# A column mean over 8192 rows: wider adds at the start, and another split of the last rows between VectorE and TensorE

## The chip, the cores and the metric

The kernel runs on one core of a Trainium2 chip. Times are device microseconds (us) of one execution. The median of three runs of the kernel before is 630.81 us (630.23 to 630.88). The execution whose trace is read here took 630.37 us, and its span, from the first to the last instruction that the profiler recorded, is 628.5 us.

## The reference

```python
def setup_inputs():
    return {"x": np.random.randn(8192, 8192).astype(np.float32)}

def reference(x: np.ndarray) -> np.ndarray:
    return np.mean(x, axis=0)
```

The input has 268.44 MB in HBM, and each number is needed once. The result is one row of 8192 numbers (32 KB).

## The kernel before, in words

**Tiles.** The 8192 rows are 64 groups of 128 rows (`G` is 64, `P` is 128). A group fills one slot of 128 partitions x 8192 columns of fp32. The tile `bufs` has six such slots. Slots 0 to 3 are landing places; slot 4 is called `both`, and slot 5 is `acc`, the accumulator. Columns are counted in blocks of 512 (`F`), so a group has 16 blocks. A small tile `early` holds 6 blocks.

**Loads.** SyncE (SP) issues every load, in program order, on one queue (line 52). Groups come in pairs: one DMA of 8.39 MB fills two neighbouring slots with 64 KB for each partition (`load_rows`). Pair `g` goes to slots `u` and `u + 1`, `u = (g + 2) % 4`, so that two pairs can be in flight or in use. The first pair goes straight to slots 4 and 5. A load into a slot waits for the add that read the slot last. The first six blocks of group 60 are loaded ahead of their turn, into `early`: two blocks as the first DMA of all, four more behind pair 4 (`load_early`). Helper `load` makes every second load wait besides for the loads eight and seven places earlier (`over`).

**Adds.** VectorE works in the order of the program. For pairs 2 and 4 there is one double add, `sums2 += two slots`, 16384 columns wide, which treats `both` and `acc` as one. After pair 4, `acc += both`. From pair 6 on, every pair has two adds of 8192 columns: `both = slot + slot`, then `acc += both`. Pair 58 is the last. An add that waits for a load has a no-op in front of it on ScalarE, or for two adds in eight on GpSimd, which waits for the load and for the add ahead (line 75), so that VectorE waits for a single semaphore. GpSimd adds the early blocks into `acc` after pairs 24 and 32 (line 110).

**The last four groups** come one by one and in pieces. For groups 60 and 61, VectorE adds blocks 6 to 15 to `acc` (5120 columns each). Group 62 comes as blocks 0 to 5 and 6 to 15; VectorE adds blocks 6 to 11 of it (3072 columns). Group 63 comes in four pieces, of 8, 4, 3 and 1 blocks. The names are `r60` to `r63`.

**The sum over partitions** is TensorE's (line 154). A matmul with a 128x32 tile of 1/8192 sums 512 columns over the partitions and adds the result to a PSUM bank. Block `i` goes to bank `i // 4`, and in it to column group `q = i % 4` of the array (32 of its 128 columns), by `tile_position`. What was not added on VectorE is given to TensorE as it is: `blocks(r62, 0, 6)` are six matmuls, one for each block. The last four blocks (2048 columns) are treated in another way: `chunks(row, 0, 3)` are four matmuls of 384 columns, one for each column group, with three quarters of these blocks' columns block by block, into bank 3; `chunks(row, 3, 4)` are four of 128 columns into bank 4. TensorE takes its matmuls in the order of the list `sums`, and the first matmul that has to wait for something holds the rest.

**The end.** ScalarE copies banks 0, 1, 2 and 3 to SBUF (line 167) and issues the store of bank 0 behind the first copy. VectorE copies bank 4 (line 177). SyncE stores banks 1 and 2, then banks 3 and 4 (line 170). Between these, SyncE has no-ops that wait for things that are long done (`landed`), so that the program's end needn't wait for all of them at once. A last no-op on VectorE waits for the first store (`hold`).

Of the kernel before, what the change touches and what calls it, by code (L numbers as in the profile page):

```python
# [9 lines left out]
def kernel(  # L10
# [5 lines left out]
    nc = tc.nc  # L16
    f32 = mybir.dt.float32
    M, N = x.shape
    P = nc.NUM_PARTITIONS
    F = 512  # L20
# [3 lines left out]
    sync = mybir.DependencyInfo(mybir.DependencyClass.Sync, mybir.DependencyReason.DATA)  # L24
# [6 lines left out]
    acc = bufs[:, U - 1, :]  # L31
    ones = sb.tile([P, 32], f32, name="ones")
    E = 6
# [2 lines left out]
    warm = sb.tile([P, 32], f32, name="warm")  # L36
    nc.gpsimd.memset(ones[:], 1.0 / M)  # L37
    ready = sb.tile([P, 1], f32, name="ready")
    set_up = tc.keep_in_program_order(
        nc.gpsimd.tensor_add(out=ready[:], in0=ones[:, 0:1], in1=ones[:, 1:2])).ins  # L40
    banks = [psp.tile([P, F], f32, name=f"bank{b}") for b in range(5)]

    loads = []

    def landed(*inss):

        nop = tc.keep_in_program_order(nc.sync.nop()).ins
        for o in inss:
            tc.add_manual_dep(nop, o.name, sync, reason="SyncE waits")

    def load(dst, src):
        ins = tc.keep_in_program_order(nc.sync.dma_start(out=dst, in_=src)).ins  # L52
        k = len(loads)
        over = loads[k - 8:k - 6] if k >= 8 and k % 2 == 0 else []
        tc.declare_no_dep(ins, group="loads", keep=over, reason="the reader of the buffer waited")
        for o in over:
            tc.add_manual_dep(ins, o.name, sync, reason="covers the next load too")
        tc.add_to_no_dep_group("loads", ins)
        loads.append(ins)
        return ins  # L60

    def rows(g, n=1):
        return x[g * P:(g + n) * P, :]

    def load_rows(g, u, n):
        return load(bufs[:, u:u + n, :], rows(g, n).rearrange("(p j) c -> p j c", j=n))
# [3 lines left out]
    def add(dst, a, b, dmas):  # L70

        ins = tc.keep_in_program_order(nc.vector.tensor_add(out=dst, in0=a, in1=b)).ins  # L72
        if dmas:
            waiter = nc.scalar if len(adds) % 8 > 1 else nc.gpsimd
            nop = joins[waiter] = tc.keep_in_program_order(waiter.nop()).ins  # L75
            for o in dmas + adds[-1:]:
                tc.add_manual_dep(nop, o.name, sync, reason="the no-op waits")
            for group in ("loads", "adds"):
                tc.declare_no_dep(ins, group=group, reason="the no-op waited")
            tc.add_manual_dep(ins, nop.name, sync, reason="waits for both at once")  # L80
        elif adds:
            tc.declare_no_dep(ins, group="loads", reason="the add ahead waited")
        tc.declare_no_dep(ins, group="early", reason="the no-op waited, or the add behind it")
        tc.add_to_no_dep_group("adds", ins)
        adds.append(ins)

    def load_early(lo, hi):
        load(early[:, lo * F:hi * F], rows(G - 4)[:, lo * F:hi * F])
# [6 lines left out]
    for g in range(2, G - 4, 2):  # L95
        u = (g + 2) % 4
        dma = load_rows(g, u, 2)
        if g < 6:
            add(sums2, sums2, bufs[:, u:u + 2, :], [dma] + first)
            first = []  # L100
            if g == 4:
                load_early(2, E)
                add(acc, acc, both, [])
            continue
        add(both, bufs[:, u, :], bufs[:, u + 1, :], [dma])
        add(acc, acc, both, ahead)
        ahead = []
        if g in (24, 32):
            cols = slice(0, 2 * F) if g == 24 else slice(2 * F, E * F)
            ins = tc.keep_in_program_order(nc.gpsimd.tensor_add(  # L110
                out=acc[:, cols], in0=acc[:, cols], in1=early[:, cols])).ins
            tc.add_to_no_dep_group("early", ins)
            ahead = [ins]

    r60, r61, r62, r63 = [bufs[:, (G - 4 + 2 + j) % 4, :] for j in range(4)]
    cols = slice(E * F, N)
# [2 lines left out]

    for lo, hi in [(0, 6), (6, 16)]:  # L120
        dma = load(r62[:, lo * F:hi * F], rows(G - 2)[:, lo * F:hi * F])
    cols = slice(6 * F, 12 * F)
    add(acc[:, cols], acc[:, cols], r62[:, cols], [dma])
    for lo, hi in [(0, 8), (8, 12), (12, 15), (15, 16)]:
        load(r63[:, lo * F:hi * F], rows(G - 1)[:, lo * F:hi * F])
# [3 lines left out]
    def blocks(row, lo, hi):  # L129
        for i in range(lo, hi):  # L130
            sums.append((i // 4, i % 4, row[:, i * F:(i + 1) * F]))

    def chunks(row, lo, hi):
        for q in range(4):
            cols = row[:, 12 * F:].rearrange("p (j q w) -> p q j w", j=4, q=4)[:, q, lo:hi, :]
            sums.append((3 + lo // 3, q, cols))
# [1 line left out]
    blocks(r62, 0, 6)  # L138
    blocks(acc, 0, 6)
    blocks(r61, 0, 6)  # L140
    chunks(r62, 0, 3)
    chunks(acc, 0, 3)
    blocks(r63, 0, 6)
    blocks(acc, 6, 12)
    blocks(r63, 6, 12)
    chunks(r62, 3, 4)
    chunks(acc, 3, 4)
    chunks(r63, 0, 3)
    chunks(r63, 3, 4)
    for n, (b, q, cols) in enumerate(sums):  # L150
        dst = banks[b][32 * q:32 * q + 32, :]
        if b > 2:
            dst = dst.rearrange("p (j w) -> p j w", w=W)[:, :cols.shape[1], :]
        summed = tc.keep_in_program_order(nc.tensor.matmul(  # L154
            out=dst,
# [10 lines left out]
    def copy(dst, src):  # L166
        return tc.keep_in_program_order(nc.scalar.copy(out=dst, in_=src)).ins  # L167

    def store(engine, dst, src):
        return tc.keep_in_program_order(engine.dma_start(out=dst, in_=src)).ins  # L170

    copy(res[:, 0, :], banks[0][:])
    s0 = store(nc.scalar, out[:4 * F].rearrange("(q c) -> q c", q=4), res[0:P:32, 0, :])
    for b in (1, 2):
        copy(res[:, b, :], banks[b][:])
    copied = copy(fin[:, :3 * W], banks[3][:, :3 * W])
    ended = nc.vector.tensor_copy(out=fin[:, 3 * W:], in_=banks[4][:, :W]).ins  # L177
    landed(*joins.values())
    landed(loads[-6], set_up)
    landed(*loads[-5:-3])  # L180
    s1 = store(nc.sync, out[4 * F:12 * F].rearrange("(b q c) -> q b c", q=4, c=F), res[0:P:32, 1:3, :])
    landed(copied)
    store(nc.sync, out[12 * F:].rearrange("(j q w) -> q j w", j=4, q=4),
          fin[0:P:32, :].rearrange("q (j w) -> q j w", w=W))
    landed(*loads[-3:-1])
    landed(loads[-1], s0)
    landed(s1, summed)
    landed(ended)
    hold = tc.keep_in_program_order(nc.vector.nop()).ins
    tc.add_manual_dep(hold, s0.name, sync, reason="VectorE ends late")  # L190


# [28 lines left out]
```

## Time and profile before

| | |
|---|---|
| median of three runs | 630.81 us (630.23 to 630.88) |
| the profiled execution's own time | 630.37 us |
| its span | 628.5 us |
| VectorE (DVE) busy | 530.0 us, 84% of the span, 61 instructions |
| TensorE (PE) busy | 15.9 us, 3% |
| ScalarE (ACT), GpSimd (POOL) busy | 3.7 us, 7.3 us |
| read from HBM | 268.44 MB, 427 GB/s over the span |

The page of the profile has busy times, a strip of 40 slices of 15.7 us each, the DMA queues, the chain of work that ended last, and the costliest groups of instructions. Engine names are PE (matmuls), PEld (weight loads), DVE, ACT, POOL and SP; a `q` behind a name is the engine's sequencer, with its waits and DMA issues. A matmul of fp32 is recorded as two, so that 60 matmuls of the program are 120 in the trace.

### The profile page before, as it was taken

What the parts mean: (1) busy time and instruction counts of PE and PEld (TensorE: products, weight loads), DVE (VectorE), ACT (ScalarE), POOL (GpSimd) and SP (SyncE); (2) the same over time, 40 slices, a digit from 0 to 9 for tenths busy, and PEclk for the clock granted to TensorE, in tenths of its full rate; (3) what the DMA queues carried; (4) which work ended last, traced back from release to release, by engine and by line L of the source; (5) the groups of instructions that cost most, each with busy time, mean ns of one, the idle gap of its engine ahead of it and who ended that gap; (6) DMA issues with size and microseconds to landing.
All of it is one profiled execution on the core that took longest, in us unless ns stands there. A gap on an engine that the chain in (4) does not pass through costs nothing.

```text
span 628.5 us, 466 instructions
## 1 busy us (share of the span) xinstructions
PE 15.9 (3%) x120; PEld 4.9 (1%) x120; DVE 530.0 (84%) x61; ACT 3.7 (1%) x6; POOL 7.3 (1%) x8
## 2 busy tenths in 40 slices
PE   0000000000000000000000000000000000000037
PEld 0000000000000000000000000000000000000002
DVE  0028999999888898888988899988889888898895
ACT  0000000000000000000000000000000000000001
POOL 0000000000000000010000200000000000000000
PEclk9999999999999999999999999999999999999999
DMA  8999999999999999999999999999999999999996
GB/s 371 463 400 430 437 467 400 467 400 467 400 467 400 467 400 467 400 467 400 467 400 467 400 467 400 467 400 467 400 467 401 463 405 463 405 463 405 432 418 254
DMA packets 5802, 268.50 MB, mean 427 GB/s; under 512 B 652, under 2 KB 668, under 8 KB 1064
## 3 DMA queue, kind: packets, MB, share of 16 engines
q1 hardware_dynamic: 5792, 268.46, 98.9%
q8 instruction: 1, 0.02, 0.0%
q10 hardware_dynamic: 8, 0.01, 0.0%
q14 instruction: 1, 0.01, 0.0%
HBM read 268.44 MB, written 0.03 MB: 427 GB/s over the span
## 4 chain that ended last, share of the span: by engine, by line
DMA 67%; DVE 28%; another core or an unknown queue 3%; PE 1%; SPq 0%; issue 0%; ACTq 0%; POOLq 0%
DMA bufs<-in_x_dram 67%; DVE bufs L72 28%; PE bank L154 1%; SPq L52 0%; ACTq L75 0%; DVE fin L177 0%; POOLq L75 0%
## 5 line engine op out<-in xcount | busy, mean ns | idle before, releaser
L72 DVE TENSOR_TENSOR bufs<-bufs 128x8192 f32<-128x8192 f32 (+3 forms) x60 | 529.7, 8828 | 90.8 <-POOLq L75 54.2
L154 PE MATMUL bank<-bufs,ones 128*32 128x512 f32 (+2 forms) x120 | 15.9, 588 | 609.5 <-DMA bufs<-in_x_dram 608.9
L110 POOL TENSOR_TENSOR bufs<-bufs,early 128x1024 f32<-128x1024 f32 (+1 forms) x2 | 6.8, 3414 | 350.1 <-DVE bufs L72 350.1
L154 PEld LDWEIGHTS bank<-bufs,ones 128*32 128x32 f32 x120 | 4.9, 118 | 620.3 <-issue 616.5
L167 ACT COPY bufs<-bank 128x512 f32<-128x512 f32 x3 | 1.8, 585 | 620.8 <-PE bank L154 620.8
L177 DVE COPY fin<-bank 128x128 f32<-128x128 f32 x1 | 0.3, 291 | 5.0 <-PE bank L154 5.0
L93 ACT ACT_TABLE_LOAD x1 | 1.3, 1283 | 0.7 <-PEq L205 0.7
L167 ACT COPY fin<-bank 128x384 f32<-128x384 f32 x1 | 0.5, 478 | 0.5 <-PE bank L154 0.5
L93 ACT COPY warm<-ones 128x32 f32<-128x32 f32 x1 | 0.2, 218 | 0.0
L40 POOL TENSOR_TENSOR ready<-ones 128x1 f32<-128x1 f32 x1 | 0.2, 193 | 0.1
L37 POOL MEMSET ones<- 128x32 f32 x1 | 0.1, 124 | 0.3 <-POOLq L205 0.3
L205 POOL MEMSET const-bfloat16-1.0<- 128x1 bf16 x1 | 0.1, 101 | 0.0
L205 POOL MEMSET const-uint8-127<- 128x1 uint8 x1 | 0.1, 101 | 0.0
L205 POOL MEMSET const-float32-0.0<- 128x1 f32 x1 | 0.1, 98 | 0.2 <-issue 0.2
L205 POOL MEMSET const-float32-1.0<- 128x1 f32 x1 | 0.1, 98 | 0.0
## 6 DMA issues: line engine op xcount, KB each, us to landing
bufs<-in_x_dram SPq DMA_DIRECT2D x2, 2560.0 KB, 16.6
bufs<-in_x_dram SPq DMA_DIRECT2D x1, 4096.0 KB
bufs<-in_x_dram SPq DMA_DIRECT2D x1, 2048.0 KB, 20.8
bufs<-in_x_dram SPq DMA_DIRECT2D x1, 1536.0 KB
early<-in_x_dram SPq DMA_DIRECT2D x1, 1024.0 KB, 62.4
bufs<-in_x_dram SPq DMA_DIRECT2D x1, 1024.0 KB, 22.9
bufs<-in_x_dram SPq DMA_DIRECT2D x1, 768.0 KB, 24.2
early<-in_x_dram SPq DMA_DIRECT2D x1, 512.0 KB, 3.4
```

The lines of the kernel that those rows point to most:

```text
L37: nc.gpsimd.memset(ones[:], 1.0 / M)
L40: nc.gpsimd.tensor_add(out=ready[:], in0=ones[:, 0:1], in1=ones[:, 1:2])).ins
L72: ins = tc.keep_in_program_order(nc.vector.tensor_add(out=dst, in0=a, in1=b)).ins
L93: tc.keep_in_program_order(nc.scalar.copy(out=warm[:], in_=ones[:]))
L110: ins = tc.keep_in_program_order(nc.gpsimd.tensor_add(out=acc[:, cols], in0=acc[:, cols], in1=early[:, cols])).ins
L154: summed = tc.keep_in_program_order(nc.tensor.matmul(out=dst, lhsT=ones[:], rhs=cols, start=all(k[:2] != (b, q) for k in sums[:n]), stop=a ...
L167: return tc.keep_in_program_order(nc.scalar.copy(out=dst, in_=src)).ins
L177: ended = nc.vector.tensor_copy(out=fin[:, 3 * W:], in_=banks[4][:, :W]).ins
L205: nc = _bacc.Bacc("TRN2", target_bir_lowering=False, num_devices=1)
```

## The change

In the first part, pairs 2, 4 and 6 are added at double width, and `acc += both` follows pair 6. The four early blocks that came behind pair 4 come as two loads, blocks 2 and 3 behind pair 4, blocks 4 and 5 behind pair 6.

In the last part, VectorE adds blocks 12 to 15 of group 62 to `acc` (2048 columns) instead of blocks 6 to 11. TensorE gets blocks 6 to 11 of group 62 as six matmuls instead of the eight `chunks` of it, so it has 58 matmuls instead of 60, and it takes them in another order. The store of banks 3 and 4 no longer lists ScalarE's copy among its own waits (a no-op ahead of it waits for that copy), one no-op no longer waits for GpSimd's first add, and VectorE's last no-op waits for the store of banks 1 and 2 instead of the store of bank 0.

```diff
-        if g < 6:
+        if g < 8:
             add(sums2, sums2, bufs[:, u:u + 2, :], [dma] + first)
             first = []
-            if g == 4:
-                load_early(2, E)
+            if g > 2:
+                load_early(g - 2, g)
+            if g == 6:
                 add(acc, acc, both, [])
             continue
...
-    cols = slice(6 * F, 12 * F)
+    cols = slice(12 * F, N)
     add(acc[:, cols], acc[:, cols], r62[:, cols], [dma])
...
     blocks(r62, 0, 6)
     blocks(acc, 0, 6)
     blocks(r61, 0, 6)
-    chunks(r62, 0, 3)
+    blocks(r62, 6, 12)
+    blocks(acc, 6, 8)
+    blocks(r63, 0, 8)
+    blocks(acc, 8, 12)
     chunks(acc, 0, 3)
-    blocks(r63, 0, 6)
-    blocks(acc, 6, 12)
-    blocks(r63, 6, 12)
-    chunks(r62, 3, 4)
     chunks(acc, 3, 4)
+    blocks(r63, 8, 12)
     chunks(r63, 0, 3)
     chunks(r63, 3, 4)
...
-    landed(loads[-6], set_up)
+    landed(loads[-6])
...
-    store(nc.sync, out[12 * F:].rearrange("(j q w) -> q j w", j=4, q=4),
+    ins = store(nc.sync, out[12 * F:].rearrange("(j q w) -> q j w", j=4, q=4),
           fin[0:P:32, :].rearrange("q (j w) -> q j w", w=W))
+    tc.declare_no_dep(ins, copied, reason="the no-op waited")
...
-    tc.add_manual_dep(hold, s0.name, sync, reason="VectorE ends late")
+    tc.add_manual_dep(hold, s1.name, sync, reason="VectorE ends late")
```

More of the change, by code (lines that the diff above doesn't have):

```diff
@@ L38 @@
     ready = sb.tile([P, 1], f32, name="ready")
-    set_up = tc.keep_in_program_order(
-        nc.gpsimd.tensor_add(out=ready[:], in0=ones[:, 0:1], in1=ones[:, 1:2])).ins
+    tc.keep_in_program_order(
+        nc.gpsimd.tensor_add(out=ready[:], in0=ones[:, 0:1], in1=ones[:, 1:2]))
     banks = [psp.tile([P, F], f32, name=f"bank{b}") for b in range(5)]
```

## The prediction

> **What bounds the kernel now.** I read the strip of slices first, because it tells where the stream of loads is not full.
>
> ```profile
> DVE  0028999999888898888988899988889888898895
> DMA  8999999999999999999999999999999999999996
> GB/s 371 463 400 430 437 467 400 467 400 467 400 467 400 467 400 467 400 467 400 467 400 467 400 467 400 467 400 467 400 467 401 463 405 463 405 463 405 432 418 254
> ```
>
> The DMA engines are busy in every slice but the first and the last. A pair of groups lands every 19.35 us (161.91, 200.60, 239.31: 38.70 for two), 433 GB/s. So the middle gives nothing, unless a load is issued too late; a gain or loss comes from the first microseconds or from what follows the last loads. The second view is the groups of instructions, kept apart by shape.
>
> ```profile
> L72 DVE TENSOR_TENSOR bufs<-bufs 128x8192 f32<-128x8192 f32 x55 | 480.9, 8743 | 45.1 <-ACTq L75 34.8 <-POOLq L75 8.8
> L72 DVE TENSOR_TENSOR bufs<-bufs 128x16384 f32<-128x16384 f32 x2 | 34.5, 17226 | 45.4 <-POOLq L75 45.4
> L72 DVE TENSOR_TENSOR bufs<-bufs 128x5120 f32<-128x5120 f32 x2 | 11.0, 5492 | 0.2
> L72 DVE TENSOR_TENSOR bufs<-bufs 128x3072 f32<-128x3072 f32 x1 | 3.4, 3358 | 0.1
> ```
>
> A pair costs VectorE 17.4 us of 19.35, so it waits for loads; the 5120 and 3072 columns at the end stand back to back with almost no idle time before them. The third view is the end of the chain of waits.
>
> ```profile
> 597.98 0.03 issue
> 598.01 20.82 DMA bufs<-in_x_dram
> 618.83 0.04 issue
> 618.87 4.67 PE bank L154 x38
> 623.54 0.00 issue
> 623.54 1.50 PE bank L154 x18
> 625.04 0.01 issue
> 625.05 0.41 PE bank L154 x4
> 625.47 0.02 issue
> 625.49 0.29 DVE fin L177
> ```
>
> TensorE starts on group 63's first eight blocks at 618.87 and is busy to 625.46. The other pieces of group 63 landed at 621.32 (blocks 8 to 11), 623.20 (the 384-wide chunks) and 623.83 (the last block), by the trace's record of landings. So at 623.83 all data is there, and TensorE is 1.6 us behind. The timeline of weight loads shows why.
>
> ```profile
> 618.87 0.16 PEld L154 LDWEIGHTS bank<-bufs,ones 128*32 128x32 f32 x8 [1.66 <-DMA bufs<-in_x_dram]
> 620.51 0.22 PEld L154 LDWEIGHTS bank<-bufs,ones 128*32 128x32 f32 x8 [0.64 <-DVE bufs L72]
> 624.80 0.70 SPq L170 DMA_DIRECT2D out_dram<-bufs  x1
> 625.92 0.54 SPq L170 DMA_DIRECT2D out_dram<-fin  x1
> ```
>
> At 620.51 it waits for VectorE: `acc` blocks 6 to 11 come from the 3072-column add, which ends at 620.46. That wait falls on column groups 2 and 3. The starts of single matmuls in the trace give the price: a column group takes 0.858 us for 512 columns (two records 0.429 apart), 0.646 for 384, 0.218 for 128, and the four work side by side. Groups 2 and 3 have to do, from 620.51: two blocks of `acc` and two of group 63 (3.43), two 128-wide chunks (0.44), one 384-wide (0.65), one 128-wide: the last starts at 625.05 and the chain ends at 625.44. That is the trace's own end within 0.02 us. Groups 0 and 1 have one block less in each of the two rows.
>
> **The change, the end.** VectorE's add has 2048 columns instead of 3072. From the rows above, 1024 columns cost (5492 - 3358) / 2 = 1067 ns, so it takes 2.29 us and ends at 617.10 + 2.29 = 619.39. TensorE's list up to 618.87: the first eighteen matmuls are the same; then six blocks of group 62 instead of eight 384-wide chunks. Column groups 2 and 3 are free from 614.75 and take two each (to 616.47), 0 and 1 one each (to 616.45). `acc` blocks 6 and 7 wait for VectorE's add of group 61, which ends at 617.00, and are done at 617.95. All of that is hidden by the wait for 618.83; without that cover, the later of these would cost 0.9 us. From 618.87 on, the four column groups now have the same work:
>
> - two blocks of group 63 and one of `acc`, with 0.02 for the start: 2.60, to 621.47;
> - `acc` chunks of 384 and 128, ready since 619.39: 0.86, to 622.33;
> - group 63's blocks 8 to 11, landed at 621.32: 0.86, to 623.19;
> - its 384-wide chunks, landed at 623.20: start at 623.24, to 623.89;
> - its 128-wide chunks, landed at 623.83: their last record starts at 624.00 and ends at 624.27.
>
> So TensorE goes from 1.6 us behind to just in time, 625.44 to 624.27, and the last loads become the bound. What is late next are the stores. Bank 2 is complete at 623.35; ScalarE copies it in 0.585 us (to 623.98), and the store of banks 1 and 2 is issued from 624.01 to 624.71 instead of from 624.80. Bank 4's copy on VectorE ends at 624.61. The last store stands behind the other on SP's queue: 624.71, and two waits of 0.06 each as in the trace of before (625.81 and 625.86), gives 624.79 to 624.87. Before, it was issued at 625.92, 0.14 after VectorE's copy. I take 624.80, 1.12 earlier: the bounds are 624.64 (right behind VectorE) and 624.95. The store itself, its landing and the end of the program took 628.50 - 625.92 = 2.58 us and stay. The wait taken off the last store belongs to these 0.06 us steps. VectorE's last no-op now waits for the store of banks 1 and 2, which landed 0.86 before the last one (626.78 and 627.64): hidden, and nothing is queued behind it but the end; if the two came together it would cost the 0.3 us from VectorE's copy to the end of its drain. The dropped wait for GpSimd was over at 1.13 us.
>
> **The change, the start.** The number of columns added does not change. Three double adds, then `acc`: 17.2 us for pair 6 instead of 2 x 8.7, a gain of 0.2 us for VectorE that is lost in its waits: at 142.61 it is waiting for a load (1.46 us idle). Pair 6's add starts with its landing, at 83.2, and ends at 100.4 instead of 97.4; the load of pair 10, which waits for that, is issued 3.0 us later. By pair 14, which lands at 161.9, the 1.9 us that VectorE gains with each pair has made that up. The early load split in two has 256 packets of 4 KB (159 ns each in the first load) instead of 128 of 8 KB (309 ns): on each of 16 engines 16 x 159 - 8 x 309 = 72 ns. That lies on the path, since the stream is full: +0.07 for all landings. SP's second issue (0.4 us) stands in its 19 us wait for VectorE, the shift of `over` by one load waits for landings long past (the last load waits for group 60's, 594.4), and group 61's no-op moves from ScalarE (38 ns) to GpSimd (43 ns), ahead of nothing.
>
> The Trainium skill speaks against such a split: in "DMA: Bandwidth & Descriptors", section "Anatomy of one DMA", each DMA has about 2 us of fixed cost, and "Rules for kernel authors" wants at least 1 MiB in one. By that rule, as an estimate, the extra DMA would cost 2 us and turn the sum into +1.0. The rows decide against it: the last two pieces of group 63, 768 and 256 KB, land 0.63 us apart, and 256 KB at 433 GB/s are 0.61, so that a queued load pays at most 0.02.
>
> **The sum.** -1.12 at the last store and +0.07 for the packets: -1.05. Span 628.50 to 627.45, the profiled execution 630.37 to 629.32. That execution was 0.44 under the median; the same saving from 630.81 gives 629.76, and I predict 629.7. The three runs of before lie 0.65 apart, and about 0.2% (1.26 us) is what a measurement of this kernel can tell from no change.
>
> **The rivals.**
>
> *The late engine.* One of the 16 DMA engines runs 0.97 us behind the rest from 485.3 on, when it moved 8 KB of instructions between two of its packets (the other 15 landed their last piece by 623.13). This delays every landing at the end. If the other number of instructions keeps that transfer off the loads, the saving is 1.05 + 0.97 = 2.0 (628.8). Against it: the list of instructions moves by one add and one load, some 20 us, and there is stream everywhere. 8%.
>
> *A gap in the stream at the start, the slower side.* Pair 6 is issued at 60.52, and in front of it there is now half the early load, landing at 63.84 instead of 65.03: a lead of 3.3 us. Pair 10 is issued at 100.45, the load in front lands at 103.92: 3.5. The smallest leads of before are 4.5 and 4.4 (79.89 to 84.33), and pair 8 then landed 19.52 after pair 6, at most 0.17 of a gap. If a load needs L us from issue to be ready, the loss is (L - 3.3) + (L - 3.5), up to 2.1 at L = 4.45, 631.9 with the saving; it decides from L = 3.9 on. For it: no lead under 4.4 is in the trace. Against it: the first load's packets move 1.0 us after its issue, and a landing is signalled 0.75 after the last packet, so that about 1.8 is enough. The floor is no loss: an earlier issue can't make a full stream faster. 10%.
>
> *TensorE at half speed.* Its matmuls came 0.853 apart in a column group until 613.0, 5.1 us after the first, and 0.429 from then on (the clock row of the page stays at full). If the pauses at 616.5 and 617.95 put it back to the slow pace at 618.87, every step of the list doubles, about +4.2, or half that if the pace returns within the burst: 631.9 to 633.9. Against it: pauses of 0.64 and 0.96 us are there before, at the same place, without that. 8%.
>
> **How the numbers follow.** The forecast, the last load bounds the end, has 74%. Its saving is 0.7 to 1.5: 0.15 for the store's step, 0.07 for packets, and up to 0.44 because I don't know what made the median longer than the profiled run; if it lies in TensorE's lag, it goes too. Half of that lies beyond 1.26. Faster: 37 + 8 = 45%. Within 0.2%: 37 and 3 from small gaps, 40%. Slower: 7 + 8 = 15%. The range goes from the late engine's 628.8 to the largest gap and the milder half-speed case, 631.9.
>
> **What would show it.** In the changed profile: a 2048-column add of 2.29 us; no wait for VectorE on TensorE after 618.9; the last matmuls within 0.5 us of the last landing; the last store's issue near 624.8, right behind the other. Pairs 6, 8, 10 and 12 landing 19.3 to 20.8 apart would clear the start; a DMA slice between 60 and 110 us under 9 would condemn it. I am wrong if TensorE still ends near 625.4, or if the landings move by more than 0.1.

## The result, and the profile after

The changed kernel takes 628.58 us (628.35 to 630.86, eight executions) against 630.51 (629.89 to 631.10) for the kernel before on the same chip: the ratio is 0.9975 (0.9963 to 0.9986), faster by 0.25%. On another chip it was 629.34, ratio 0.9986 (0.9976 to 0.9995). The profiled execution took 628.35 us; its span is 626.52 instead of 628.50.

The strip of slices of the changed kernel:

```profile
DVE  0028979999988998888988899988899888998894
DMA  9999999999999999999999999999999999999997
GB/s 377 460 402 428 475 435 402 469 402 469 402 469 402 464 406 460 410 448 423 418 452 402 469 402 469 402 469 402 469 402 469 402 469 402 464 406 460 395 426 295
```

The stream is full in every slice but the last, the first slices included: no gap came in at the start. Pairs 8, 10 and 12 landed 20.57, 19.36 and 19.35 us after the pair ahead (an early load lies between 6 and 8). The three wide adds end at 100.3 us, in slice 7; from there VectorE works without a pause to 135.4. By shape:

```profile
L72 DVE TENSOR_TENSOR bufs<-bufs 128x16384 f32<-128x16384 f32 x3 | 51.7, 17225 | 48.6 <-POOLq L75 45.3 <-ACTq L75 3.4
L72 DVE TENSOR_TENSOR bufs<-bufs 128x2048 f32<-128x2048 f32 x1 | 2.3, 2292 | 0.1
```

The wide add takes 17.2 us as before, and 2048 columns take 2.29 us, as worked out. The end of the chain of waits (start, duration, what it was):

```profile
597.02 20.89 DMA bufs<-in_x_dram
617.95 5.49 PE bank L155 x64
623.46 0.29 DVE fin L178
```

And the timeline of the same end (start, duration, and in brackets the idle time ahead with what ended it):

```profile
617.95 0.16 PEld L155 LDWEIGHTS bank<-bufs,ones 128*32 128x32 f32 x8 [1.68 <-DMA bufs<-in_x_dram]
622.32 0.16 PEld L155 LDWEIGHTS bank<-bufs,ones 128*32 128x32 f32 x8 [0.78 <-DMA bufs<-in_x_dram]
622.96 0.17 PEld L155 LDWEIGHTS bank<-bufs,ones 128*32 128x32 f32 x8 [0.48 <-DMA bufs<-in_x_dram]
623.13 0.70 SPq L171 DMA_DIRECT2D out_dram<-bufs  x1
623.94 0.54 SPq L171 DMA_DIRECT2D out_dram<-fin  x1
```

Each weight load that waits in this stretch waits for a DMA; the wait for VectorE at 620.51 is gone. From 617.95 to the end, TensorE takes 5.49 us where before it took 6.59 (618.87 to 625.46). The span is shorter by 1.98 us, in two parts, both read from the two traces:

| | before | after | |
|---|---|---|---|
| last load landed | 623.83 | 622.91 | -0.92 |
| from there to the last store's issue | 2.09 | 1.03 | -1.06 |
| from there to the end of the span | 2.58 | 2.58 | 0 |

The second part was forecast at -1.12. The first was forecast at +0.07, and it needed the experiments. The trace's DMA queues, from 484.5 to 486.5 us, show where to look (packets, MB, share of 16 engines). Before:

```profile
q1 hardware_dynamic: 16, 1.05, 123.2%
q14 instruction: 1, 0.01, 1.0%
```

After, in the same window:

```profile
q1 hardware_dynamic: 16, 1.05, 121.1%
```

The 8 KB of instructions that put one of the 16 DMA engines late in the kernel before is not there any more. In the changed kernel it moves at 626.3 us, behind the last store's landing. The chain of waits has the price. The pair whose load is issued next ahead of that place is 0.70 us longer on its way in the kernel before (start, duration), and the next pair in the chain takes 29.92 us in both kernels again:

```profile
480.30 30.63 DMA bufs<-in_x_dram
```

```profile
480.06 29.93 DMA bufs<-in_x_dram
```

### The profile page after: what moved, and what is told of

Its sections match the earlier page's. It is cut to its first block, busy times and chain, and to the rows that moved or that the text cites. A ratio compares the mean times of both kernels' runs of the same rounds, so it can differ in the third digit from the quotient of the medians.

```text
span 626.5 us, 457 instructions
## 1 busy us (share of the span) xinstructions
PE 14.6 (2%) x116; PEld 4.4 (1%) x116; DVE 528.7 (84%) x60; ACT 3.7 (1%) x6; POOL 7.4 (1%) x8
## 4 chain that ended last, share of the span: by engine, by line
DMA 70%; DVE 28%; PE 1%; SPq 0%; issue 0%; ACTq 0%; POOLq 0%
DMA bufs<-in_x_dram 70%; DVE bufs L72 28%; PE bank L155 1%; SPq L52 0%; ACTq L75 0%; DVE fin L178 0%; POOLq L75 0%
## 5 line engine op out<-in xcount | busy, mean ns | idle before, releaser
L155 PE MATMUL bank<-bufs,ones 128*32 128x512 f32 (+2 forms) x116 | 14.6, 604 | 608.8 <-DMA bufs<-in_x_dram 607.8
```

Of the source, the lines that this page charges most:

```text
L155: summed = tc.keep_in_program_order(nc.tensor.matmul(out=dst, lhsT=ones[:], rhs=cols, start=all(k[:2] != (b, q) for k in sums[:n]), stop=a ...
```

## The experiments

**1. The kernel before, again.** No edit.

> The kernel of before, unchanged, once more. The profile of before has a transfer of 8 KB of instructions at 485.3 us that sets one DMA engine 0.97 us behind; the profile of the changed kernel has that transfer at 626.3 us, after the last load. If the place of the transfer follows from the instructions of the kernel, this profile shows it near 485 us again and its last load lands near 623.8. If it is chance, it may be elsewhere, and the last load lands near 622.9. By both the tail is the same: TensorE ends 1.6 us behind the last landing (2.5 if the engine is not late and everything else is). Ratio 1.000.

630.43 us, ratio 1.0002 (0.9993 to 1.0011). The instruction transfer is again at 485.3 us and the last load lands at 623.79, so that its place belongs to the program. But the span is 629.19, and the timeline and the table of windows (us, then busy time of PE, PEld, DVE, ACT, POOL, granted clock, DMA share, GB/s) show something new:

```profile
618.86 7.27 PE L154 MATMUL bank<-bufs,ones 128*32 128x512 f32 x68 [0.97 <-DMA bufs<-in_x_dram]
```

```profile
612.00:618.50 6.50, 4.58 (x36) 1.15 (x32) 6.40 (x2) 0.00 (x0) 0.00 (x0) 1.00 0.99 418
618.50:621.90 3.40, 3.04 (x16) 0.85 (x20) 1.94 (x1) 0.59 (x1) 0.00 (x0) 0.50 0.99 403
621.90:626.00 4.10, 4.10 (x56) 1.78 (x48) 0.00 (x0) 1.21 (x3) 0.00 (x0) 1.00 0.07 25
```

TensorE was granted half its clock from 618.5 to 621.9 us, in the middle of its last burst, and ended at 626.13 instead of 625.44. It had paused for 1.31 us, and was 0.6 us into a second pause, of 0.97, when the clock fell. The mean clock of a whole execution tells whether this happened: it is under 0.998 in 34 of 107 executions of the kernel before, whose median is 631.1 us; that of the other 73 is 630.1. Of the kernels with the changed end, 1 of 92 shows it.

The Trainium skill, "TensorE: Matmul & The Clock Gate", section "HAM oscillation — how this bites in real kernels", gives as the rule that TensorE must have no idle gaps over about 3.4 us. This trace differs: the clock fell after a pause of 1.31 us and within one of 0.97, in a stretch where TensorE was busy for 4.58 us of 6.50. The measurement decides: short gaps are no safeguard here. In the same stretch of the first profile of before, at full clock, the pauses were 0.64 and 0.96 us and TensorE was busy for 5.27 of 6.50; in experiment 10 pauses of 1.18 and 0.76 left the clock at full. What length or share sets it off, these runs don't tell.

**2 and 3. Each half alone.** The end only: the kernel before with VectorE's columns, TensorE's list and the waits of stores and no-op as in the changed kernel.

```diff
-    cols = slice(6 * F, 12 * F)
+    cols = slice(12 * F, N)
...
+    blocks(r62, 6, 12)
+    blocks(acc, 6, 8)
+    blocks(r63, 0, 8)
+    blocks(acc, 8, 12)
...
-    tc.add_manual_dep(hold, s0.name, sync, reason="VectorE ends late")
+    tc.add_manual_dep(hold, s1.name, sync, reason="VectorE ends late")
```

> The start of before with the end of the changed kernel. The sum of the prediction gives the end 1.12 us: a ratio of 0.998, TensorE ending 0.45 us behind the last landing, the last store's issue about 0.55 behind that. If the start is what moved the 8 KB transfer off the loads, this run has it among the loads still and the last load lands near 623.8; if the end moved it (fewer matmuls, other waits), it lands near 622.85 and the run is 2.1 us faster in all.

629.59 us, ratio 0.9987 (0.9978 to 0.9996). The last load lands at 623.87 with the transfer at 485.3, TensorE ends 0.48 behind it, and the end of the chain and SP's two stores are:

```profile
618.92 5.48 PE bank L154 x64
624.42 0.29 DVE fin L177
```

```profile
624.10 0.69 SPq L170 DMA_DIRECT2D out_dram<-bufs  x1
624.91 0.54 SPq L170 DMA_DIRECT2D out_dram<-fin  x1
```

The last store is issued 1.04 behind the last landing instead of 2.09. This is the forecast's own case, with its own numbers (624.10 and 624.91 where 624.01 and 624.80 were worked out).

The start only: the changed kernel with the end of before.

```diff
-        if g < 6:
+        if g < 8:
...
-            if g == 4:
-                load_early(2, E)
+            if g > 2:
+                load_early(g - 2, g)
+            if g == 6:
                 add(acc, acc, both, [])
```

> The start of the changed kernel with the end of before. By the sum: 0.07 us slower for the packets of 4 KB, nothing else, ratio 1.000, TensorE 1.6 us behind the last landing. If the start moved the 8 KB transfer: landings 0.9 earlier and a run 0.9 us faster. By the rival of a gap in the stream: pairs 6 and 10 landing late by up to 1 us each, 2 us slower in all.

630.37 us, ratio 0.9998 (0.9990 to 1.0007): no gain to be seen. Yet the trace has the transfer gone from 485 us and the last landing at 622.93, 0.90 earlier. Two things take that back. TensorE now ends 1.62 behind the landing, because the wait for VectorE is still there; and the transfer, at 625.75, falls into the last store, which lands 2.18 us after its issue instead of 1.72.

So the start moves the transfer, and the earlier landing counts in full only together with the changed end.

**4. The changed kernel, again.** No edit.

> The changed kernel, unchanged, once more. If the place of the 8 KB transfer follows from the instructions, no engine is late and the last load lands near 622.9, as in its first profile; if it is chance, it may come among the loads, and then the landing is near 623.9 and the span 627.4, as the sum of the prediction has it. Ratio 0.9975 or 0.9983.

629.34 us, ratio 0.9986 (0.9976 to 0.9995). In the profiled execution, of 628.89 us, the transfer is at 626.8, again behind everything. The last landing is at 623.45, because another DMA engine fell 0.6 us behind near 103 us, where one packet took 3219 ns instead of 2418. Five of the eleven executions took 630.35 to 630.57 us, and none of these was profiled; more on them below.

**5. One instruction more on VectorE.** Why does the transfer move? The changed start has one VectorE instruction less: pair 6 has one add instead of two. So the list gets it back, by an add of nothing to the path: one column set to zero ahead of the loads.

```diff
+    spare = sb.tile([P, 1], f32, name="spare")
+    tc.keep_in_program_order(nc.vector.memset(spare[:], 0.0))
```

> The changed kernel with one more instruction on VectorE at the start, a memset of one column. Four profiles had the 8 KB transfer at 485.3 us where VectorE's list has as many instructions as before (before, the same again, end of the changed kernel alone) and behind the last load where it has one less (changed kernel twice, start alone). If VectorE's list decides, the transfer is among the loads again, near 485, one engine is 0.97 us late to the end, the last load lands near 623.85 and the span is near 627.5: the whole extra gain over the prediction is gone. If the loads' order decides, it stays near 626 and the span near 626.5.

The transfer is back, in the trace's DMA queues from 484.5 to 486.5 us:

```profile
q1 hardware_dynamic: 16, 1.05, 123.1%
q14 instruction: 1, 0.01, 1.0%
```

One instruction of no weight brings it back. In all 14 profiles the transfer is near 485 us whenever VectorE's list has the length of before (before, 1, 2, 5, 7), and behind the last load whenever it is one shorter (after, 3, 4, 6, 8 to 12). Why one instruction moves it so far is not shown.

The time is 629.27 us (628.98 to 629.67), ratio 0.9977 (0.9968 to 0.9986). The profiled execution, of 629.67 us, has its last landing at 624.07, 1.16 later than the changed kernel, and its span is 627.71. But this delay is not the transfer's. Two packets near 103 us took 3676 and 3171 ns instead of 2418, and pair 10 landed at 124.10 us instead of 122.95: the 1.15 were there long ahead of 485 us. The pair in flight there is not late:

```profile
481.22 29.94 DMA bufs<-in_x_dram
```

The engine that carried the 8 KB fell behind here too (its next packet took 3081 ns), but another was later still. So this run shows what decides the transfer's place. What it costs is shown by the four other profiles that have it near 485 us. There the pair in flight takes 30.63, 30.88, 30.73 and 30.70 us instead of 29.93 (before, 1, 2, 7), and the slowest DMA engine of the last load lands 0.70 to 0.96 behind the next one. Where the transfer comes behind the last load, that distance is 0.01 to 0.13, but for experiment 4 (0.61, the packet at 103 us). The times agree: experiment 8, on the same chip and with the shorter list, took 628.74 us, 0.53 less than this one.

**6. VectorE's last no-op waits for the first store again.**

```diff
-    tc.add_manual_dep(hold, s1.name, sync, reason="VectorE ends late")
+    tc.add_manual_dep(hold, s0.name, sync, reason="VectorE ends late")
```

> The changed kernel with VectorE's last no-op waiting for the first store again, as before. The prediction costs this edit at nothing. By the start-alone run, where VectorE went to its end code right after its copy and the last store landed 0.47 us later than elsewhere: the 8 KB transfer then comes 1.1 us after VectorE's end, at 624.9, in the middle of the last store (issued at 623.95, landing at 625.7), and the span grows by 0.3 to 0.5 us. By the prediction: no change.

629.71 us, ratio 0.9989 (0.9980 to 0.9998). The last landing is where it should be, at 622.97. But the transfer moves at 624.9 us, while the last store (issued at 624.00) is under way; that store lands 2.38 us after its issue instead of 1.72, and from its issue to the end of the span it is 3.23 instead of 2.58. SP's wait for it, here and in the changed kernel (line, what it waited for: us in total, times, longest):

```profile
SPq L218 <- DMA out_dram<-fin: 1.0, 1, 1.0
```

```profile
SPq L218 <- DMA out_dram<-fin: 0.3, 1, 0.3
```

The edit of the no-op, costed at nothing, is worth 0.65 us: VectorE reaches its end later, and the transfer, which follows the end of VectorE's last branch by 1.09 us in experiment 3 and in the changed kernel and by 1.36 here, starts when the last store has landed. On the same chip, experiment 8 has the changed kernel's hold and took 628.74 us.

**7. TensorE's order alone.** Before, with VectorE's 3072 columns, and the list changed so that the wait for them stands behind all of group 63's first blocks.

```diff
     chunks(r62, 0, 3)
-    chunks(acc, 0, 3)
-    blocks(r63, 0, 6)
-    blocks(acc, 6, 12)
-    blocks(r63, 6, 12)
     chunks(r62, 3, 4)
+    blocks(r63, 0, 8)
+    blocks(acc, 6, 12)
+    chunks(acc, 0, 3)
     chunks(acc, 3, 4)
+    blocks(r63, 8, 12)
```

> Before, with its start and its split between VectorE and TensorE, and only the order of TensorE's list made like the changed one (all eight first blocks of group 63 ahead of acc 6 to 11, acc's chunks ahead of the later pieces of group 63). Adding the 0.858, 0.646 and 0.218 us per column group: the last record of TensorE starts 0.35 us earlier than before, so the order alone gives a third of the 1.1 us and the other split of group 62 the rest. Ratio 0.9994. If the order gave it all, 1.1 us, 0.998.

Slower: 631.90 us, ratio 1.0021 (1.0011 to 1.0032). The timeline and the windows:

```profile
618.53 9.11 PE L154 MATMUL bank<-bufs,ones 128*32 128x512 f32 x68 [3.20 <-DMA bufs<-in_x_dram]
```

```profile
617.60:624.40 6.80, 5.87 (x30) 1.49 (x34) 2.51 (x1) 1.06 (x2) 0.00 (x0) 0.50 0.66 267
624.40:628.00 3.60, 3.24 (x44) 1.57 (x36) 0.29 (x1) 1.18 (x3) 0.00 (x0) 1.00 0.00 0
```

Without the work it had ahead of group 63, TensorE pauses for 3.20 us from 615.3, is granted half its clock from 617.6 to 624.4, and ends at 627.64. Nine of ten executions show the lower mean clock, so the loss is the clock's. The one at 0.999 took 630.02, against the 630.1 of before at full clock: whether the order alone gives the expected 0.35 us is not shown. In the changed kernel, the six extra blocks of group 62 keep TensorE busy in that stretch (its pauses are 1.01 and 0.77 us), and its clock stayed at full.

**8. The store's waits.** After, with the last store listing ScalarE's copy again and the no-op waiting for GpSimd's first add again.

```diff
-    landed(loads[-6])
+    landed(loads[-6], set_up)
...
-    ins = store(nc.sync, out[12 * F:].rearrange("(j q w) -> q j w", j=4, q=4),
+    store(nc.sync, out[12 * F:].rearrange("(j q w) -> q j w", j=4, q=4),
...
-    tc.declare_no_dep(ins, copied, reason="the no-op waited")
```

> The changed kernel with the last store listing ScalarE's copy among its waits again, and the no-op waiting for GpSimd's first add. The prediction counts these as steps of 0.06 us on SP: the last store's issue 0 to 0.06 us later, ratio to the changed kernel 1.000. A theory that gives these edits more than 0.1 us falls if it doesn't show in the distance from the first store's issue on SP to the last's (0.81 us in the changed kernel).

628.74 us, ratio 0.9971 (0.9960 to 0.9983). SP's two stores start at 622.98 and 623.85, 0.87 apart instead of 0.81: the edit is worth 0.06 us at most, and no time shows it.

**9. A shorter lead.** After, with the four early blocks as one load behind pair 6, so that pair 6 follows pair 4 directly.

```diff
-            if g > 2:
-                load_early(g - 2, g)
             if g == 6:
+                load_early(2, E)
                 add(acc, acc, both, [])
```

> The changed kernel with the four early blocks as one load behind pair 6, so that nothing lies between pair 4 and the load of pair 6. That load is then issued 2.0 us before the landing in front of it (60.4 and 62.4) instead of 3.3. By the estimate of the prediction (packets move 1.0 us after an issue, a landing is signalled 0.75 after its last packet, 1.8 needed) no gap: pair 6 lands 19.35 after pair 4, and the last load 0.04 earlier than in the changed kernel. By the rival of a gap, a load needs up to 4.4 us: pair 6 lands up to 2.4 us late, and everything after it.

629.25 us (628.97 to 629.47), ratio 0.9979 (0.9970 to 0.9988). The chain of waits at pair 6:

```profile
60.32 21.83 DMA bufs<-in_x_dram
82.15 0.03 ACTq L75
82.21 17.23 DVE bufs L72
```

Pair 6 is issued at 60.32, 2.05 us ahead of pair 4's landing at 62.37, and lands 19.78 after it; in the changed kernel it lands 19.35 behind the landing in front (63.67 and 83.02). A lead of 2.05 thus loses 0.4 us, and by that a load needs an estimated 2.45 us from its issue to the landing in front. The changed kernel's leads, 3.27 us for pair 6 and 3.26 for pair 10 (issued at 100.33, 103.59 in front), have 0.8 to spare.

**10 to 12. Bank 1 stored first.** In all these kernels the last store stands behind the other on SP's queue. So bank 1 was stored by itself as soon as it is copied; 11 is the changed kernel beside it on the same chip, and 12 the same edit on another chip.

```diff
-    s1 = store(nc.sync, out[4 * F:12 * F].rearrange("(b q c) -> q b c", q=4, c=F), res[0:P:32, 1:3, :])
+    s2 = store(nc.sync, out[4 * F:8 * F].rearrange("(q c) -> q c", q=4), res[0:P:32, 1, :])
+    s1 = store(nc.sync, out[8 * F:12 * F].rearrange("(q c) -> q c", q=4), res[0:P:32, 2, :])
...
+    landed(s2)
```

> The changed kernel with the store of banks 1 and 2 split: bank 1 is stored as soon as ScalarE has copied it (621.4), bank 2 where both were stored (623.1). The single store keeps SP for 0.70 us, to 623.83, and the last store is issued at 623.94 though VectorE's copy ended at 623.75. If SP is what the last store waits for, a smaller store frees it sooner: the last store's issue 0.10 to 0.15 us earlier, span 626.4, beyond what the times can tell. If not, no change, and an extra store may cost SP time at the end.

> The changed kernel once more, one look: 6 of its 19 executions so far were 1.9 us longer than its best, at a full clock, and none of the 22 where VectorE's list is one longer with the same end. If this is such an execution (about one in three), its trace shows whether the 1.9 us lie ahead of the last landing (a late engine or a gap at the start) or behind the last store (the 8 KB transfer of VectorE in the end of the program). Otherwise as in the first profile.

> The kernel with bank 1 stored first, once more: 6 of its 12 executions were 1.8 to 2.4 us longer than its best, at a granted clock of 0.999 or 1.000, as were 6 of 20 of the changed kernel. If the profiled execution is one of those, its trace settles where they lose. Theory one, TensorE at half speed in the final burst without its slack of before: the last landing is near 623, TensorE ends 2 us later than the 0.5 us behind it that the other profiles show, weight loads 0.64 apart. Theory two, VectorE's 8 KB transfer in the way of the end: TensorE ends near 623.6 and the time from the last store's issue to the end grows from 2.6 to 4.5 us. Theory three, a gap at the start or a late engine: the last landing itself is near 625. If it is an undisturbed one, the question stays open.

Experiment 10 took 629.36 us, ratio 0.9985 (0.9974 to 0.9995), experiment 12 628.44, ratio 0.9980 (0.9967 to 0.9993); the changed kernel in experiment 11 took 628.61. The last store is issued 0.39 behind TensorE's end in both instead of 0.55: 0.15 us gained in the trace, nothing that the times can show. No version clearly beats the changed kernel.

**What stays open.** Some executions take 630.1 to 631.0 us where the others of the same kernel take 628.0 to 629.4: 6 of 20 of the changed kernel and 9 of 22 with bank 1 first, at a mean clock of 0.999 or 1.000 in all but one. In experiment 6, two of 11 stand out so (630.9); in experiments 2, 5, 8 and 9 none of 39. None fell on a profile. They decide whether the changed kernel's median is 628.6 or 629.3; their cause was not found.

## Why the prediction was right or wrong

**The time.** 629.7 was forecast, in 628.8 to 631.9. By the ratio, the 630.81 of before becomes 629.2 on the first chip and 629.9 on the second, both in the range; the median of 628.58 itself lies 0.2 below it. The first ratio is beyond 0.2%, the second not: the chances of 45 and 40% sat on either side of the line on which the result lies. That 629.2 lies within the range is owed to its lower edge, the 628.8 of the rival that had 8%. The prediction also named a sign of being wrong, landings that move by more than 0.1; they moved by 0.92, so by its own sign its account of the loads was wrong. The sum, -1.05 of span, was too small by 0.93, and the experiments say where.

**What bounds the kernel, and the end: right.** TensorE was behind because of the wait for VectorE, and with 2048 columns and the new list it ends 0.48 behind the last landing (0.44 was worked out). The last store's issue gained 1.06 us instead of 1.12, because SP's first store came at 623.13, 0.22 behind the landing, where 0.18 was worked out, and the step between the stores was 0.81 where 0.79 was. Experiment 2 shows this part alone. What comes late next is also as forecast: the store stands behind the other store, which experiment 10 loosens by 0.15.

**The start: the term of +0.07 was the one that failed.** The sum had only the 4 KB packets there. The landing came 0.92 earlier, for the reason of the first rival, *the late engine*, which had 8% and a time of 628.8. The step that put it so low is "the list of instructions moves by one add and one load, some 20 us, and there is stream everywhere". One add less did not move the transfer by 20 us but by 141, to the far end; experiment 5 shows that this one VectorE instruction decides. Of the 0.92, 0.70 comes with the transfer (30.63 and 29.93). The other 0.22 was there before it: pair 46 landed at 471.52 us before and at 471.29 after. That is scatter. In the 11 profiles without a late packet or a gap at the start it landed from 471.10 to 471.52, and the packets' 0.07 is lost in that too. So the rival had the cause right, and its size, 2.0 against the 1.98 measured, in part by luck: it put the late engine at 0.97, the distance to the other engines, where the landing moved by 0.70, and the scatter made up for most of it.

**"Hidden", for the no-op: wrong.** The prediction asked who waits behind the no-op, and nothing does. It didn't ask what VectorE's end sets off. With the transfer at the end, the older hold costs 0.65 us (experiment 6). With the transfer at 485 us, as in the kernel before, there was nothing to collide with: the two edits are worth their sum only together.

**The gap in the stream: right in its conclusion, wrong in its estimate.** The wide adds shift pair 10 without a loss. But a load needs about 2.45 us (experiment 9), not the 1.8 worked out from the first load; the rival's deciding point, L = 3.9, is still far. One term of the 1.8 was also misread: in the trace of before, the first load's last packet ends at 3.80 us and the landing is at 4.16, 0.36 later and not 0.75. By that reading even less would have been enough, so it is the way of working it out that failed. What fills the rest is not shown; in experiment 9 no engine stood still, but 15 of pair 6's first 16 packets took 2.58 to 3.13 us each instead of 2.42.

**TensorE at half speed: a real mechanism, on the other side.** The one profile of before showed none of it, and the rival was put in the changed kernel. But it strikes the kernel before, in a third of its executions, and with the changed end it is all but gone (none of 11 in experiment 2). This is a second part of the gain in the medians that the sum didn't have: the 630.81 that it started from stands 0.7 above the kernel's median at full clock, 630.1.

**The store's waits, the extra load: right.** 0.06 at most (experiment 8), and SP's second issue for the early blocks cost nothing that a landing shows. Nor did the second DMA itself: its first half, 512 KB, landed 1.23 us behind pair 4 (62.44 and 63.67), where 433 GB/s give 1.21. The 2 us set against it came from a section that is headed as the path of DMAs issued by GpSimd; these loads are SyncE's.

## What to carry to other kernels

When a stream of loads is full from end to end, look at the slowest DMA engine of the last load and at what else it carried; one instruction more or less on another engine can decide where that falls. Find the place in the stream where the landings first come late, before a late end is put down to one cause. Before an edit at an engine's end is costed at nothing, ask what the end of its list sets off, not only who waits behind it. And when a list of work is cut ahead of a final burst, see what the pause does to the clock, in several executions and not in one profile.

## What the runs showed of the hardware

- Instructions come by DMA, on a queue of their own: 8 KB that follow VectorE's list move in 0.33 us between two packets of the loads, and the next 64 KB packet takes 3.08 us instead of 2.42. In a full stream the engine that carried them stays late for the 138 us that are left: it lands the last load 0.70 to 0.96 us behind the next engine (before, 1, 2, 7).
- One slow packet does the same: 3.22 us instead of 2.42 near 103 us put every later landing back by 0.6 us (experiment 4), 3.68 us by 1.15 (experiment 5). What slowed them is not shown.
- If the transfer of instructions meets the last 8 KB store, the store's landing takes 2.18 or 2.38 us instead of 1.72.
- TensorE's clock fell to half for 3.4 us after a pause of 1.31 us and 0.6 of a second one (experiment 1), and for 6.8 when it had paused for 2.2 us (experiment 7).
- A load queued 2.05 us ahead of the landing in front leaves a gap of 0.4 us. The Trainium skill, "DMA: Bandwidth & Descriptors", section "Specifications", gives about 0.6 us of latency to the first byte on this path; in this trace the first load's packets move 1.0 us after its issue, and what a queue must have ahead to run without a gap is more than either.
